# Half of an output projection's columns for one head group as seven block products, placed singly between plain pieces

## The chip, the cores and the metric

One core of one Trainium2 chip runs one transformer layer in fp32. The metric is the device time of one execution in microseconds. Three timed executions of the kernel before took 1103.21, 1103.28 and 1104.04 us; the median is 1103.28 us.

## The reference

Two groups of eight heads (width 128 each) feed one output projection, whose 2048 rows are the 1024 features of the forgetting heads (FoX) and the 1024 of the stick-breaking heads. The projection adds onto the residual stream, and a gated feed-forward network (FFN) with a short convolution follows.

```python
h = rms_norm(x, attn_norm)
p = h @ w_in                                   # q, k, v and forget gates of group A; q, k, v of group B
out_a = forgetting_attention(qa, ka, va, c)    # softmax with cumulative log-forget bias, causal
out_b = stick_breaking_attention(qb, kb, vb)
merged = concat(rms_norm(out_a, out_norm_fox), rms_norm(out_b, out_norm_sb))
x = x + merged @ w_out                         # 256 tokens, 2048 -> 2048
x = x + conv_ffn(rms_norm(x, ffn_norm))        # up 2048 -> 2 * 5632, causal conv of width 3, SiLU gate, down
```

## The kernel before, in words

**Products.** There are 256 tokens (two tiles of 128). Every fp32 weight block of 128 x 2048 elements per piece (four row blocks of 128, 512 columns) is loaded raw (`w_raw`, three buffers), rounded to a high part by ScalarE (`w_hi`, L207) and its remainder taken by VectorE (`w_lo`, L208), two buffers each in this stage. The left side (`oT`, `hT`) is held in two such parts too, and a product is the sum of high x high, low x high and high x low. `in_three` (L221) issues these matmuls, L229 in the profile: the ones with `w_hi` first, then those with `w_lo`. A plain piece of the output projection has 16 and then 8 matmuls of 128 x 512, over both token tiles.

**Output projection.** The loop at L781 goes over the two head groups, and in each over four column groups of 512. `token_major` makes one column group in two pieces of four heads each, into one accumulator `acc` (PSUM pool `psa`). Then two VectorE instructions (L803, one for each token tile) scale the accumulator by the token's RMS factor `rg` and add it onto the residual `x`. After each piece `step()` advances up to two waiting generators: the last stick-breaking heads are still running while the forgetting group's columns are projected, and `next_rows` transposes finished residual columns for the FFN (`ps_x`, L138).

**A head's rows on the engines.** A head's weights are transposed on TensorE (`ps_p`, L607) into a bank of the PSUM pool `pss` (tag "s", two banks, which the heads' scores `ps_s` and `ps_z` share). ScalarE copies them out in two instructions (L610, L611), and VectorE takes the low part from the same bank (L612, `w<-ps_p`). One step later TensorE multiplies by the values (`ps_o`, L593, L594).

**Block products elsewhere.** The down projection of the FFN already works in seven products for a 2 x 2 block of (token tiles, column groups) and two row halves: `down_in_seven`, with `bank_a`, `bank_b` and `bank_c` as one-bank accumulators, a summed weight `w_sum` (L1005), and weights that a GpSimd transfer adds onto others in place (L975, `accum_op`). Each of its products has 12 matmuls of 128 x 512.

**What sets the order.** TensorE runs in the order written. In the attention stage, VectorE, ScalarE and the queues are ordered by a scheduler; weight loads and splits get a priority of 200 (`AHEAD`) instructions. Each engine then runs its own instructions strictly in that order.

Of the kernel before, what the change touches and what calls it, by code (L numbers as in the profile page):

```python
# [2 lines left out]

# [11 lines left out]
P = 128  # L15
D = 2048
S = 256
# [28 lines left out]
def hybrid_layer(  # L46
# [31 lines left out]
    def f32(t):  # L78
        return t.bitcast(F32)
# [48 lines left out]
        nc.tensor.transpose(pp[:, :n], rows, ident[:n, :n])  # L128
        dve.tensor_copy(dst, pp[:, :n])

    hT = big.tile([P, KT, 2, S], F32R, name="hT")

    def transposed_split(k, g, n=2):

        ps = psb.tile([P, 2, S], F32, name="ps_x", tag="t")
        for j in range(n):
            for t in range(NT):
                nc.tensor.transpose(  # L138
                    ps[:, j, t * P : (t + 1) * P], xt[t][:, (k + j) * P : (k + j + 1) * P], ident
                )  # L140
        for j in range(n):
            i = k + j
            act.activation(hT[:, i, 0, :], ps[:, j, :], AF.Identity, scale=g[:, i : i + 1])
        for j in range(n):
            i = k + j
            dve.scalar_tensor_tensor(
                hT[:, i, 1, :], ps[:, j, :], g[:, i : i + 1], f32(hT[:, i, 0, :]),
                op0=ALU.mult, op1=ALU.subtract,
            )

# [46 lines left out]
    def load(src):  # L197
# [2 lines left out]
        nc.sync.dma_start(raw[:, : a * b].rearrange("p (a b) -> p a b", a=a), src)  # L200
        return raw

    def split(raw, a, b):
# [3 lines left out]
        act.copy(hi[:, :n], raw[:, :n])  # L207
        dve.tensor_tensor(lo[:, :n], raw[:, :n], f32(hi[:, :n]), op=ALU.subtract)  # L208
# [9 lines left out]
    def rows_of(w, k0, n, c0, cols):  # L218
        return w[k0 * P : (k0 + n) * P, c0 : c0 + cols].rearrange("(k p) c -> p k c", p=P)
# [14 lines left out]
    def of_half(h, part, t):  # L234
        return h[:, part, t * P : (t + 1) * P]

    def token_major(lhs, w, k0, nk, c0, cols):

        acc = psa.tile([P, NT, 512], F32, name="acc", tag="acc")
        for k in range(0, nk, 4):  # L240
            parts = weights(rows_of(w, k0 + k, 4, c0, cols), 4, cols)
            in_three(
                [acc[:, t, :cols] for t in range(NT)], parts, 4,
                lambda i, part, t: of_half(lhs(k + i), part, t), k == 0, k + 4 == nk,
            )
            step()
        return acc

    def from_features(acc, parts, kh, n=8, low_first=False):

        hi, lo = parts

        def high(k, i, j):
            nc.tensor.matmul(  # L254
                acc[:, j, :], hi[:, i, j * P : (j + 1) * P],
                hT[:, k].rearrange("p a b -> p (a b)"), start=k == 0, stop=low_first and k == KT - 1,
            )

        def low(k, i, j):
            nc.tensor.matmul(  # L260
                acc[:, j, S:], lo[:, i, j * P : (j + 1) * P], hT[:, k, 0, :],
                start=False, stop=not low_first and k == KT - 1,
            )
# [23 lines left out]
    with ExitStack() as actx:  # L287
# [7 lines left out]
        late = actx.enter_context(tc.tile_pool(name="late", bufs=1))  # L295

        def project(c0, cols):
            return token_major(lambda k: hT[:, k], wi, 0, KT, c0, cols)

        def scaled(dst, ps, t):  # L300
            act.activation(dst, ps, AF.Identity, scale=rstd1[:, t : t + 1])
# [35 lines left out]

        oT = [late.tile([P, 2, S], F32R, name=f"oT{h}") for h in range(NH)]  # L340
        vA_low = late.tile([P, WF], F32R, name="vA_low", tag="two_heads")
        done = []
        ssq = [late.tile([P, S], F32, name=f"ssq{i}") for i in range(2)]

        def attended(po, h, g, group):

            if len(done) == NH:

                two = late.tile([P, 2, 2, S], F32R, name="oT89", tag="two_heads")
                oT.extend([two[:, 0], two[:, 1]])  # L350
                oT.extend(late.tile([P, 2, S], F32R, name=f"oT{i}") for i in range(NH + 2, 2 * NH - 4))
                oT.extend(hT[:, KT - 4 + i] for i in range(4))
            done.append(group * NH + h)
            assert done[-1] == len(done) - 1
            o = oT[group * NH + h]
            act.activation(o[:, 0, :], po, AF.Identity, scale=g[:, h : h + 1])
            dve.scalar_tensor_tensor(
                o[:, 1, :], po, g[:, h : h + 1], f32(o[:, 0, :]), op0=ALU.mult, op1=ALU.subtract
            )
            if h == 0:  # L360
                act.activation(ssq[group], po, AF.Square)
            else:
                sq = tmp.tile([P, S], F32, name="osq", tag="t1", bufs=3)
                act.activation(sq, po, AF.Square)
                dve.tensor_tensor(ssq[group], ssq[group], sq, op=ALU.add)
# [19 lines left out]
        def opening():  # L385
# [37 lines left out]
            def multiply(c, i, n, high):  # L423
                hi, lo = (p[:, i : i + n] for p in parts[c])
                order = [(j, l, hi) for j in range(n) for l in range(2)] if high else [(j, 0, lo) for j in range(n)]
                for m, (j, l, r) in enumerate(order):
                    for t in range(NT):
                        nc.tensor.matmul(  # L428
                            acc[:, t, :], of_half(hT[:, 2 * c + i + j], l, t), r[:, j, :],
                            start=high and c == i == m == 0, stop=not high and c == 7 and m == n - 1,  # L430
                        )

# [93 lines left out]
        step()  # L526


        vA = (at.tile([P, WF], F32R, name="vA"), vA_low, at.tile([P, WF], F32, name="vA_t1"))

        def values(dst, acc):
            hi, lo, rest = dst
# [189 lines left out]
        def sb_head(h, qT, kT, v):  # L722
# [31 lines left out]
                yield  # L754
            attended(weighted(v, slice((h % 4) * HD, (h % 4 + 1) * HD), (w, w1)), h, g_sb, 1)

        for half in range(2):
            qT = sb_queries(half)
            kT = sb_keys(half)
# [14 lines left out]
        ss2 = const.tile([P, NT, 4], F32, name="ss2")  # L774

        def next_rows(c):
            for k in range(4 * c, 4 * c + 4, 2):
                transposed_split(k, g_ffn)
            yield

        for group in range(2):  # L781
            rg = const.tile([P, NT], F32, name=f"rg{group}")
            if group == 1:
                finish()
            for c in range(4):
                acc = token_major(lambda k: oT[group * NH + k], wo, group * NH, NH, 512 * c, 512)
                if group == c == 0:
                    assert scored[: NH + 4] == list(range(NH + 4))
                    x2 = big.tile([P, NT, D], F32, name="x2", tag="x2")
                    xt[:] = [x2[:, t, :] for t in range(NT)]  # L790
                    for t in range(NT):
                        nc.gpsimd.dma_start(xt[t], xf[t * P : (t + 1) * P, :])
                if c == 0:
                    pg = psb.tile([P, NT], F32, name="pg", tag="t")
# [5 lines left out]
                    rsqrt(rg, pg, 1.0 / WF, NT)  # L800
                for t in range(NT):
                    xs = xt[t][:, c * 512 : (c + 1) * 512]
                    dve.scalar_tensor_tensor(  # L803
                        xs, acc[:, t, :], rg[:, t : t + 1], xs, op0=ALU.mult, op1=ALU.add
                    )
# [369 lines left out]
```

## Time and profile before

| | |
|---|---|
| median of three | 1103.28 us |
| the profiled execution | 1103.81 us, of which the span from the first to the last instruction is 1102.0 us |
| TensorE busy | 1096.5 us (99%) |
| VectorE busy | 877.7 us (80%) |
| ScalarE busy | 701.9 us (64%) |
| granted TensorE clock | 1.000 |
| chain that ended last | TensorE 99% |
| stretch of the output projection | about 299.9 to 394.9 us of the span |

A profile row of a timeline reads: start, length, engine, line, operation, output <- input, shape, count, and in brackets how long the engine was idle before it and what ended that. The length of a row of several matmuls runs to the modelled end of the last, so the pitch from one matmul to the next is read from starts.

### The profile page before, as it was taken

To read this page: it belongs to the slowest core of one execution; us is meant where nothing else is said; L and a number is where in the kernel's file an instruction comes from. 1 tells how busy PE (TensorE), PEld (TensorE's weight loads), DVE (VectorE), ACT (ScalarE), POOL (GpSimd) and SP (SyncE) were. 2 spreads that over 40 slices of the span, in tenths; PEclk is the share of its full clock that TensorE was granted. 3 is DMA by queue.
4 is the path that set the end of the run, shared out by engine and by line. 5 is a ranking of instruction groups with operands and counts; after the bars stand their busy time and mean duration, and the time that the engine had idled before them with its cause. 6 is when DMAs were issued, how large, how long until landed. Compare 5 with 4: busy or idle time off the path is not lost.

```text
span 1102.0 us, 14826 instructions
## 1 busy us (share of the span) xinstructions
PE 1096.5 (99%) x5868; PEld 951.2 (86%) x5868; DVE 877.7 (80%) x941; ACT 701.9 (64%) x879; POOL 44.4 (4%) x46
## 2 busy tenths in 40 slices
PE   9999999999999999999999999999999999999998
PEld 7998888888888888888888888888888888888887
DVE  5655777975775677689889988889798889889896
ACT  6544556664653566677767776767676777677753
POOL 0000000000000000000000010100000010100010
PEclk9999999999999999999999999999999999999999
DMA  8776654576545396558989597986979689997985
GB/s 288 171 244 230 188 156 153 153 231 197 184 161 186 112 317 196 181 191 209 288 223 312 191 234 264 261 269 177 315 209 303 217 218 282 241 266 198 322 208 177
DMA packets 179407, 245.89 MB, mean 223 GB/s; under 512 B 4432, under 2 KB 119018, under 8 KB 179082
## 3 DMA queue, kind: packets, MB, share of 16 engines
q1 hardware_dynamic: 162458, 209.67, 58.6%
q0 software_dynamic: 16560, 34.75, 16.8%
q8 instruction: 46, 0.75, 0.3%
q10 hardware_dynamic: 320, 0.53, 0.1%
q14 instruction: 23, 0.19, 0.0%
HBM read 242.82 MB, written 2.11 MB: 222 GB/s over the span
## 4 chain that ended last, share of the span: by engine, by line
PE 99%; DMA 0%; DVE 0%; SPq 0%; issue 0%
PE pu L254 34%; PE acc L229 22%; PE pu L260 18%; PE bank_a L229 10%; PE bank_b L229 5%; PE bank_c L229 2%; PE acc L428 2%; PE acc L1053 1%; PE ps_x L138 1%; PE ps_o L593 1%; PE bank_a L1053 1%; PE ps_p L607 0%; DMA w_raw<-in_w_in_dram 0%; PE ps_o L594 0%; PE ps_h L307 0%; PE ps_s L522 0%
## 5 line engine op out<-in xcount | busy, mean ns | idle before, releaser
L208 DVE TENSOR_TENSOR w_lo<-w_raw,w_hi 128x2048 fp32r<-128x2048 f32 (+1 forms) x196 | 439.6, 2246 | 129.5 <-ACT w_hi L207 128.6
L207 ACT CAST w_hi<-w_raw 128x2048 fp32r<-128x2048 f32 (+1 forms) x196 | 367.3, 1877 | 235.9 <-PE acc L229 66.6
L254 PE MATMUL pu<-hT,w_hi 128*128 128x512 f32 x1664 | 394.0, 390 | 0.0
L254 PEld LDWEIGHTS pu<-hT,w_hi 128*128 128x128 f32 x1664 | 310.3, 188 | 63.2
L260 PEld LDWEIGHTS pu<-hT,w_lo 128*128 128x128 f32 x1664 | 211.9, 191 | 7.0
L260 PE MATMUL pu<-hT,w_lo 128*128 128x256 f32 x1664 | 215.1, 283 | 0.0
L229 PE MATMUL acc<-w_hi,hT 128*128 128x512 f32 (+1 forms) x576 | 124.5, 368 | 0.0
L229 PEld LDWEIGHTS acc<-w_hi,hT 128*128 128x128 f32 x576 | 101.5, 188 | 14.3
L207 ACT CAST w_hi<-w_sum 128x2048 fp32r<-128x2048 f32 x30 | 57.3, 1909 | 44.2 <-PE pu L254 36.6
L208 DVE TENSOR_TENSOR w_lo<-w_sum,w_hi 128x2048 fp32r<-128x2048 f32 x30 | 68.7, 2290 | 20.8 <-ACT w_hi L207 20.7
L870 ACT ACTIVATE tap<-up,ccol 128x256 f32<-128x256 f32 x176 | 74.6, 495 | 0.0
L229 PE MATMUL acc<-w_lo,hT 128*128 128x512 f32 (+1 forms) x288 | 64.6, 366 | 0.0
L229 PEld LDWEIGHTS acc<-w_lo,hT 128*128 128x128 f32 x288 | 51.6, 188 | 7.5
L975 POOL DMA_DIRECT2D w_sum<-in_w_down_dram x20 | 25.7, 1284 | 797.7 <-DVE w_lo L208 786.1
L229 PE MATMUL acc<-w_hi,oT 128*128 128x512 f32 x192 | 46.0, 392 | 0.0
L229 PEld LDWEIGHTS acc<-w_hi,oT 128*128 128x128 f32 x192 | 35.7, 188 | 7.3
L229 PE MATMUL bank_a<-w_hi,g 128*128 128x512 f32 x160 | 40.0, 392 | 0.0
L229 PE MATMUL bank_b<-w_hi,s 128*128 128x512 f32 x160 | 40.0, 392 | 0.0
L229 PE MATMUL bank_a<-w_hi,s 128*128 128x512 f32 x160 | 40.0, 392 | 0.0
L229 PEld LDWEIGHTS bank_b<-w_hi,s 128*128 128x128 f32 x160 | 28.9, 189 | 5.2
L229 PEld LDWEIGHTS bank_a<-w_hi,g 128*128 128x128 f32 x160 | 28.8, 189 | 5.3
L229 PEld LDWEIGHTS bank_a<-w_hi,s 128*128 128x128 f32 x160 | 28.9, 189 | 5.2
(211 smaller groups left out, 1068.7 us busy)
## 6 DMA issues: line engine op xcount, KB each, us to landing
w_raw<-in_w_up_dram SPq DMA_DIRECT2D x88, 1024.0 KB, 7.5
w_raw<-in_w_down_dram SPq DMA_DIRECT2D x44, 1024.0 KB, 6.4
w_raw<-in_w_in_dram SPq DMA_DIRECT2D x36, 1024.0 KB, 5.4
w_sum<-in_w_down_dram POOLq DMA_DIRECT2D x20, 1024.0 KB, 9.9
w_raw<-in_w_out_dram SPq DMA_DIRECT2D x16, 1024.0 KB, 5.1
w_raw<-in_w_down_dram POOLq DMA_DIRECT2D x10, 1024.0 KB, 14.9
w_raw<-in_w_in_dram SPq DMA_DIRECT2D x12, 688.0 KB, 4.2
w_raw<-in_w_in_dram SPq DMA_DIRECT2D x6, 512.0 KB, 6.8
```

The source lines that it names most:

```text
L138: nc.tensor.transpose(ps[:, j, t * P : (t + 1) * P], xt[t][:, (k + j) * P : (k + j + 1) * P], ident)
L207: act.copy(hi[:, :n], raw[:, :n])
L208: dve.tensor_tensor(lo[:, :n], raw[:, :n], f32(hi[:, :n]), op=ALU.subtract)
L229: nc.tensor.matmul(o, lhs(i, l, t), r[:, i, :], start=starts and j == 0, stop=stops and j == 3 * n - 1, skip_group_check=more,)
L254: nc.tensor.matmul(acc[:, j, :], hi[:, i, j * P : (j + 1) * P], hT[:, k].rearrange("p a b -> p (a b)"), start=k == 0, stop=low_first and k ...
L260: nc.tensor.matmul(acc[:, j, S:], lo[:, i, j * P : (j + 1) * P], hT[:, k, 0, :], start=False, stop=not low_first and k == KT - 1,)
L428: nc.tensor.matmul(acc[:, t, :], of_half(hT[:, 2 * c + i + j], l, t), r[:, j, :], start=high and c == i == m == 0, stop=not high and c == ...
L593: nc.tensor.matmul(po, v[j][:, hs], wp[:, k], start=i == 0, stop=False)
L870: act.activation(taps[w][:, j, :], u[:, j, w : w + S], AF.Copy, scale=ccol[:, w, f : f + 1])
L975: nc.gpsimd.dma_start(mem[into][:, : nk * 512].rearrange("p (a b) -> p a b", a=nk), src, accum_op=ALU.add)
L1053: nc.tensor.matmul(o, of_half(g, l, t), r[:, i, c0 : c0 + cols], start=kh == 0 and j == 0, stop=kh == n - 1 and j == 11,)
```

## The change

For the forgetting heads, the column groups 2 and 3 (columns 1024 to 2047) are no longer made by `token_major` in four plain pieces (96 matmuls of 128 x 512). They become a 2 x 2 block (token tiles by column groups, with two halves of four heads inside) made by `in_seven`, in seven products of 12 matmuls (84). The plain pieces that are left are the forgetting heads' columns 0 and 1 and all of the stick-breaking heads' columns, and `token_major` takes one product out of the generator `seven` behind each of its pieces. The first two calls only pass (the first issues two loads), so the seven products stand behind the third to the ninth plain piece.

Seven products need sums on both sides. `block_sums` makes sums of the heads' outputs on VectorE (six instructions, in the stretch of the second half's keys), and `block_parts` splits them into high and low (two ScalarE, two VectorE instructions). On the weight side, one VectorE addition makes `w_sum` from w11 and w12, and three GpSimd transfers add w22, w22 and w21 in place. Two weight tiles are loaded into freed memory (`w_sum` where the values of the forgetting heads were, `x12` in a quarter of `hT`, which is now four tiles). Each product is accumulated in one bank of `pss`, the pool with tag "s" that the heads' `ps_z` and `ps_p` use. `in_turn` keeps the weight splits in the order of the program, and `in_order` pins the sums. Behind column group 1 of the second head group, two `next_rows` run in a chain in place of one each behind groups 0 and 1.

```diff
+    def residual(t, c, ps, factor):
+        xs = xt[t][:, c : c + 512]
+        dve.scalar_tensor_tensor(xs, ps, factor[:, t : t + 1], xs, op0=ALU.mult, op1=ALU.add)
+    def in_seven(c0, plus_rg, minus_rg):
+        w11, w12, w21, w22 = (rows_of(wo, 4 * h, 4, c0 + 512 * i, 512) for h in range(2) for i in range(2))
...
+        def product(bank, lhs, parts, to, factor=plus_rg):
+            new = bank not in banks
+            if new:
+                banks[bank] = pss.tile([P, 512], F32, name=bank, tag="s")
+            in_three([banks[bank]], parts, 4, lhs, new, True, more=not new)
+            residual(to[0], c0 + 512 * to[1], banks[bank], factor)
...
+        with tc.high_priority(offset=AHEAD):
+            for into, src in ((w, w11), (x12, w12)):
+                nc.sync.dma_start(into.rearrange("p (a b) -> p a b", a=4), src)
+        yield
+        yield
+        with tc.high_priority(offset=AHEAD):
+            parts = split(w, 4, 512)
+        in_order(dve.tensor_tensor(w, w, x12, op=ALU.add))
+        product("bank_a", of_heads(0, 0), parts, (0, 0))
+        yield
+        block_parts()
+        product("bank_c", of_heads(1, 0), weights(w21, 4, 512), (0, 0))
+        yield
+        with tc.high_priority(offset=AHEAD):
+            parts = split(w, 4, 512)
+        plus(w, w22)
+        plus(x12, w22)
+        product("bank_b", of_sums(0, 1), parts, (1, 1))
+        yield
+        product("bank_b", of_sums(1, 0), weights(w22, 4, 512), (0, 1))
+        yield
+        with tc.high_priority(offset=AHEAD):
+            parts = split(w, 4, 512)
+        plus(w, w21)
+        product("bank_a", of_sums(1, 1), parts, (0, 1), minus_rg)
+        yield
+        with tc.high_priority(offset=AHEAD):
+            parts = split(x12, 4, 512)
+        product("bank_a", of_sums(0, 0), parts, (1, 1), minus_rg)
+        yield
+        with tc.high_priority(offset=AHEAD):
+            parts = split(w, 4, 512)
+        product("bank_a", of_heads(1, 1), parts, (1, 0))
...
-            for c in range(4):
-                acc = token_major(lambda k: oT[group * NH + k], wo, group * NH, NH, 512 * c, 512)
+            for c in range(4 if group else 2):
+                acc = token_major(
+                    lambda k: oT[group * NH + k], wo, group * NH, NH, 512 * c, 512,
+                    seven,
+                )
...
-                    waiting.append(next_rows(c))
+                    if c == 1:
+                        waiting.append(chain(next_rows(0), next_rows(1)))
+                    elif c > 1:
+                        waiting.append(next_rows(c))
```

Two places show what this does to the engines' orders.

**TensorE where the first of the seven is put.** Before, behind the first piece of the forgetting heads' column group 1, two heads' weights are transposed (`ps_p`, three matmuls a head) and the next plain piece follows:

```order
L229 MATMUL acc_2963<-w_lo_2967,oT2_100 128x512 x2
L229 MATMUL acc_2963<-w_lo_2967,oT3_101 128x512 x2
L607 MATMUL ps_p_2994<-cs_70,e_2886 128x128 x3
L607 MATMUL ps_p_3003<-cs_70,e_2903 128x128 x3
L229 MATMUL acc_2963<-w_hi_3014,oT4_102 128x512 x4
L229 MATMUL acc_2963<-w_hi_3014,oT5_103 128x512 x4
```

Now the first product stands there, in `bank_a`:

```order
L245 MATMUL acc_2973<-w_hi_2976,oT_fox_101 128x512 x16
L245 MATMUL acc_2973<-w_lo_2977,oT_fox_101 128x512 x8
L626 MATMUL ps_p_3004<-cs_70,e_2891 128x128 x3
L626 MATMUL ps_p_3013<-cs_70,e_2908 128x128 x3
L245 MATMUL bank_a_3027<-w_hi_3022,oT_fox_101 128x512 x8
L245 MATMUL bank_a_3027<-w_lo_3023,oT_fox_101 128x512 x4
L245 MATMUL acc_2973<-w_hi_3043,oT_fox_101 128x512 x16
```

The plain piece moved behind it. `ps_p_3004` and `ps_p_3013` hold the two banks of the pool, and `bank_a` is the third tile asked of it: its first matmul waits for VectorE, for the instruction that reads `ps_p_3004` last (`w<-ps_p`).

**VectorE at the same place.** Before (`rs_a` and `rs_u` are small steps of the RMS factor `rg`, `e` the heads' weights before transposition):

```order
L748 TENSOR_TENSOR e<-e,masks 128x2x128 x2
L111 TENSOR_SCALAR rs_a<-pg 128x2
L208 TENSOR_TENSOR w_lo<-w_raw,w_hi 128x2048
L114 TENSOR_TENSOR rs_u<-rs_a,rs_y 128x2
L612 TENSOR_TENSOR w<-ps_p,w 128x256
L115 TENSOR_TENSOR rs_u<-rs_u,rs_y 128x2
```

Now:

```order
L767 TENSOR_TENSOR e<-e,masks 128x2x128 x2
L112 TENSOR_SCALAR rs_a<-pg 128x2
L868 TENSOR_TENSOR w_sum<-w_sum,x_2921 128x2048
L221 TENSOR_TENSOR w_lo<-w_raw,w_hi 128x2048
L115 TENSOR_TENSOR rs_u<-rs_a,rs_y 128x2
L631 TENSOR_TENSOR w<-ps_p,w 128x256
L116 TENSOR_TENSOR rs_u<-rs_u,rs_y 128x2
```

The addition for `w_sum` came in ahead of the split. The reading of `ps_p` keeps its place behind the split of a later piece's weights.

**VectorE in the second half's keys.** Before (`ssq` sums squares of the heads' outputs, `t` is the projected pair of heads):

```order
L685 TENSOR_TENSOR q_parts<-t_2470,q_parts 128x256
L208 TENSOR_TENSOR w_lo<-w_raw,w_hi 128x2048
L365 TENSOR_TENSOR ssq_108<-ssq_108,osq 128x256 x2
L284 TENSOR_TENSOR t_2554<-pu,t_2554 128x512
L678 SCALAR_TENSOR_TENSOR t_2554<-t_2554,R_1503 128x512
L208 TENSOR_TENSOR w_lo<-w_raw,w_hi 128x2048
```

Now:

```order
L704 TENSOR_TENSOR q_parts<-t_2465,q_parts 128x256
L784 TENSOR_TENSOR oT_blocks_2472<-oT_fox 128x1024
L221 TENSOR_TENSOR w_lo<-w_raw,w_hi 128x2048
L383 TENSOR_TENSOR ssq_104<-ssq_104,osq 128x256
L784 TENSOR_TENSOR oT_blocks_2474<-oT_fox 128x1024
L383 TENSOR_TENSOR ssq_104<-ssq_104,osq 128x256
L788 TENSOR_TENSOR oT_blocks_2472<-oT_blocks_2472 128x4x128
L789 TENSOR_TENSOR oT_blocks_2472<-oT_blocks_2472,oT_blocks_2474 128x4x128
L790 SCALAR_TENSOR_TENSOR oT_blocks_2474<-oT_blocks_2472,oT_blocks_2474 128x4x128
L301 TENSOR_TENSOR t_2557<-pu,t_2557 128x512
L791 TENSOR_TENSOR oT_blocks_2474<-oT_blocks_2474 128x4x128
L697 SCALAR_TENSOR_TENSOR t_2557<-t_2557,R_1498 128x512
```

The six sums of `block_sums` came in around the split and the steps of the next pair of keys.

More of the change, by code (lines that the diff above doesn't have):

```diff
@@ L2 @@
 from contextlib import ExitStack, nullcontext
+from itertools import chain
 import concourse.bass as bass
@@ L129, in columns, with new_tokens @@
         dve.tensor_copy(dst, pp[:, :n])
-    hT = big.tile([P, KT, 2, S], F32R, name="hT")
+    hT = [None] * KT
+    def new_tokens(g):
+        t = big.tile([P, 4, 2, S], F32R, name=f"hT{g}", tag=f"hT{g}")
+        hT[4 * g : 4 * g + 4] = [t[:, i] for i in range(4)]
+    for g in range(4):
+        new_tokens(g)
     def transposed_split(k, g, n=2):
@@ L206, in split @@
         n = a * b
-        act.copy(hi[:, :n], raw[:, :n])
-        dve.tensor_tensor(lo[:, :n], raw[:, :n], f32(hi[:, :n]), op=ALU.subtract)
+        with ExitStack() as turn:
+            for ins in in_turn:
+                turn.enter_context(tc.issue_after(ins.ins))
+            last = [act.copy(hi[:, :n], raw[:, :n])]
+            last.append(dve.tensor_tensor(lo[:, :n], raw[:, :n], f32(hi[:, :n]), op=ALU.subtract))
+        last_split[:] = last
+        if in_turn:
+            in_turn[:] = last
         return (
@@ L246, in token_major @@
             step()
+            next(behind, None)
         return acc
@@ L255, in high @@
                 acc[:, j, :], hi[:, i, j * P : (j + 1) * P],
[L256 removed]
+                hT[k].rearrange("p a b -> p (a b)"), start=k == 0, stop=low_first and k == KT - 1,
             )
@@ L336, in fox_rows @@
             yield
-        oT = [late.tile([P, 2, S], F32R, name=f"oT{h}") for h in range(NH)]
-        vA_low = late.tile([P, WF], F32R, name="vA_low", tag="two_heads")
+        oT_fox = late.tile([P, NH, 2, S], F32R, name="oT_fox")
+        oT = [oT_fox[:, h] for h in range(NH)]
+        vA_rest = late.tile([P, WF], F32, name="vA_rest", tag="two_heads")
         done = []
@@ L351, in attended @@
                 oT.extend(late.tile([P, 2, S], F32R, name=f"oT{i}") for i in range(NH + 2, 2 * NH - 4))
-                oT.extend(hT[:, KT - 4 + i] for i in range(4))
+                oT.extend(hT[KT - 4 + i] for i in range(4))
             done.append(group * NH + h)
@@ L755, in sb_head, with block_sums, block_parts @@
             attended(weighted(v, slice((h % 4) * HD, (h % 4 + 1) * HD), (w, w1)), h, g_sb, 1)
+        in_order = tc.keep_in_program_order
+        blocks, sums = [], []
+        def block_sums():
+            for h, tag in enumerate(("minus_c1", "blocks")):
+                blocks.append(at.tile([P, 4, S], F32, name=f"oT_blocks{h}", tag=tag))
+                some = slice(4 * h, 4 * h + 4)
+                in_order(dve.tensor_tensor(
+                    blocks[h], f32(oT_fox[:, some, 0, :]), f32(oT_fox[:, some, 1, :]), op=ALU.add
+                ))
+            a11, a21, a12, a22 = (blocks[h][:, :, t * P : (t + 1) * P] for h in range(2) for t in range(2))
+            in_order(dve.tensor_tensor(a11, a11, a21, op=ALU.subtract))
+            in_order(dve.tensor_tensor(a21, a21, a22, op=ALU.subtract))
+            in_order(dve.scalar_tensor_tensor(a22, a11, -1.0, a22, op0=ALU.mult, op1=ALU.subtract))
+            in_order(dve.tensor_tensor(a12, a12, a22, op=ALU.add))
+        def block_parts():
+            sums.extend(big.tile([P, NH, S], F32R, name="oT_sums", tag=f"hT{g}") for g in (1, 2))
+            places = [[t[:, 4 * h : 4 * h + 4] for t in sums] for h in range(2)]
+            for (hi, _), block in zip(places, blocks):
+                in_order(act.copy(hi, block))
+            for (hi, lo), block in zip(places, blocks):
+                in_order(dve.tensor_tensor(lo, block, f32(hi), op=ALU.subtract))
         for half in range(2):
             qT = sb_queries(half)
+            if half:
+                block_sums()
             kT = sb_keys(half)
@@ L779, in next_rows, with of_heads, of_sums, plus @@
             yield
-        for group in range(2):
-            rg = const.tile([P, NT], F32, name=f"rg{group}")
+        def residual(t, c, ps, factor):
[3 more added lines that the diff above has]
+            w11, w12, w21, w22 = (rows_of(wo, 4 * h, 4, c0 + 512 * i, 512) for h in range(2) for i in range(2))
+            banks = {}
+            def of_heads(h, t):
+                return lambda i, part, _: of_half(oT[4 * h + i], part, t)
+            def of_sums(h, t):
+                return lambda i, part, _: sums[part][:, 4 * h + i, t * P : (t + 1) * P]
+            def plus(into, src):
+                with tc.high_priority(offset=AHEAD):
+                    nc.gpsimd.dma_start(
+                        into.rearrange("p (a b) -> p a b", a=4), src, accum_op=ALU.add
+                    )
[5 more added lines that the diff above has]
+                residual(to[0], c0 + 512 * to[1], banks[bank], factor)
+            w, x12 = (
+                pool.tile([P, 2048], F32, name=name, tag=tag)
+                for pool, name, tag in ((at, "w_sum", "vA"), (big, "x12", "hT0"))
+            )
+            with tc.high_priority(offset=AHEAD):
[28 more added lines that the diff above has]
+            yield
+            with tc.high_priority(offset=AHEAD):
+                parts = split(w, 4, 512)
+            product("bank_a", of_heads(1, 1), parts, (1, 0))
@@ L783, in hybrid_layer @@
+        rgs = [const.tile([P, NT], F32, name=f"rg{group}") for group in range(2)]
+        minus_rg = const.tile([P, NT], F32, name="minus_rg")
+        seven = in_seven(1024, rgs[0], minus_rg)
+        in_turn.extend(last_split)
+        for group, rg in enumerate(rgs):
             if group == 1:
                 finish()
-            for c in range(4):
-                acc = token_major(lambda k: oT[group * NH + k], wo, group * NH, NH, 512 * c, 512)
+            for c in range(4 if group else 2):
+                acc = token_major(
+                    lambda k: oT[group * NH + k], wo, group * NH, NH, 512 * c, 512,
+                    seven,
+                )
```

26 lines of the change are left out of this document (15 added, 11 removed).

## The prediction

> **What bounds the kernel now.** I read the page first: busy times and the chain that ended last.
>
> ```profile
> span 1102.0 us, 14826 instructions
> PE 1096.5 (99%) x5868; PEld 951.2 (86%) x5868; DVE 877.7 (80%) x941; ACT 701.9 (64%) x879; POOL 44.4 (4%) x46
> PE 99%; DMA 0%; DVE 0%; SPq 0%; issue 0%
> ```
>
> TensorE is the bound from end to end. So a matmul taken away is worth its pitch, and any wait that TensorE gets is paid in full, since nothing later has slack to give it back. Next, whom TensorE waits for, in the whole span (columns: in total, times, longest):
>
> ```profile
> PE idle L381 <- DVE zeros L371: 1.1, 1, 1.1
> PE acc L428 <- DVE w_hi L409: 1.1, 1, 1.1
> PE ps_x L138 <- DMA x<-in_x_dram: 0.2, 1, 0.2
> ```
>
> All three lie in the first 7 us. In the output projection TensorE never waits; the change has to keep that. Then the room on the helpers there, from windows (PE, PEld, DVE, ACT, POOL busy, clock, DMA share, GB/s):
>
> ```profile
> 290.00:320.00 30.00, 30.00 (x152) 25.35 (x151) 20.12 (x25) 17.69 (x28) 0.00 (x0) 1.00 0.48 157
> 320.00:350.00 30.00, 30.00 (x139) 24.98 (x138) 19.50 (x23) 11.98 (x13) 0.00 (x0) 1.00 0.60 194
> 350.00:380.00 30.00, 30.00 (x144) 25.05 (x143) 18.95 (x22) 15.44 (x23) 0.00 (x0) 1.00 0.44 141
> ```
>
> VectorE has about 31 us free of 90, ScalarE 45. Room in sum is there; what decides is who stands behind whom.
>
> **The change part by part.** *Matmuls taken away.* Pitches come from the chain in order of time (start, length, what):
>
> ```profile
> 326.53 32.67 PE acc L229 x144
> 527.17 2.75 PE bank_a L229 x12
> ```
>
> A plain matmul takes 32.67 / 144 = 0.227 us, the 96 that go are 21.8 us. A block product of 12 matmuls takes 2.75 us in the FFN, seven are 19.25 us. The gain is 21.8 - 19.25 = 2.5 us (2.7 if the new ones run at the plain pitch).
>
> *Work added to the helpers.* From the page and the tile `w_sum`:
>
> ```profile
> L207 ACT CAST w_hi<-w_sum 128x2048 fp32r<-128x2048 f32 x30 | 57.3, 1909 | 44.2 <-PE pu L254 36.6
> L208 DVE TENSOR_TENSOR w_lo<-w_sum,w_hi 128x2048 fp32r<-128x2048 f32 x30 | 68.7, 2290 | 20.8 <-ACT w_hi L207 20.7
> L1005 DVE TENSOR_TENSOR w_sum<-w_raw x10: 2283/2284/2292, 493.5 to 1049.8; 128x2048 f32<-128x2048 f32 x10
> ```
>
> Seven splits in place of four: ScalarE 3 x 1.91 = 5.7 us, VectorE 3 x 2.29 = 6.9 us, and one weight sum of 2.28 us. In the new rhythm a plain piece (24 x 0.227 = 5.44 us) and a product (2.75 us) make 8.19 us, against two splits: 3.82 us on ScalarE, 4.58 us on VectorE. With two buffers, the high part of the next plain piece can begin when the 16 high matmuls of this one are through (3.63 us) and ends near 3.7 + 1.9 = 5.6 us, 2.6 us before it is needed; its low part begins at 5.5 us, ends at 7.8 us and is needed at 8.19 + 3.63 us. So the steady rhythm costs TensorE nothing: splits are hidden by the matmuls of the piece and product before.
>
> *The first product, bank_a.* Here the order makes a wait. This is the place in the trace of before, TensorE, then ScalarE, then VectorE:
>
> ```profile
> 319.06 0.82 PE L607 MATMUL ps_p<-cs,e 128*128 128x128 f32 x6
> 319.63 3.91 PE L229 MATMUL acc<-w_hi,oT 128*128 128x512 f32 x16
> ...
> 317.85 1.89 ACT L207 CAST w_hi<-w_raw 128x2048 fp32r<-128x2048 f32 x1
> ...
> 317.55 0.15 DVE L111 TENSOR_SCALAR rs_a<-pg 128x2 f32<-128x2 f32 x1
> 319.77 2.29 DVE L208 TENSOR_TENSOR w_lo<-w_raw,w_hi 128x2048 fp32r<-128x2048 f32 x1 [2.07 <-ACT w_hi L207]
> 321.98 0.15 DVE L114 TENSOR_TENSOR rs_u<-rs_a,rs_y 128x2 f32<-128x2 f32 x1
> 322.05 0.42 DVE L612 TENSOR_TENSOR w<-ps_p,w 128x256 fp32r<-128x256 f32 x1
> ```
>
> Up to here the two programs run alike (the same pieces of 24, the same heads). TensorE is through with `ps_p` at 319.63, and before it went on into `acc`, another pool. Now `bank_a` wants the bank of the first `ps_p`, which VectorE reads last in `w<-ps_p`. That read already ended as late as 322.47, because the split of a later piece stands ahead of it; nobody cared. Now the weight sum comes in at 317.62, fills the idle 2.07 us and ends its turn at 317.62 + 2.21 = 319.83 (2.21 us is the pitch from 319.77 to 321.98); the split starts 0.06 us later than before, `w<-ps_p` ends at 322.53, and TensorE starts about 322.6. It stands idle for 322.6 - 319.63 = 3.0 us. Lower bound: 322.47 - 319.63 = 2.8 us, if the sum cost nothing at all; upper: 3.5 us, if another half microsecond of small steps goes ahead of it. I take 3.0. Queued behind the waiting `bank_a` on TensorE is everything else, so it is paid in full. The other six products ask for a bank whose last readers (`x` additions, or a `ps_p` two pieces back) are long done.
>
> What such a gap does to the clock: the longest gap in the trace is 1.1 us (the waits above), and the granted clock is 1.00 in every window quoted. [...] A 3.0 us gap is not shown in this trace, so I keep it as a rival.
>
> *Sums of the heads' outputs.* `block_parts` stands ahead of the third product. Between the first two products lie a plain piece and two heads' `ps_o`, which take 1.1 us:
>
> ```profile
> 325.20 0.41 PE L593 MATMUL ps_o<-w,vB 128*128 128x256 f32 x2
> ...
> 326.29 3.91 PE L229 MATMUL acc<-w_hi,oT 128*128 128x512 f32 x16
> ```
>
> So the second product runs from 322.6 + 2.75 + 5.44 + 1.1 = 331.9, and the third from 331.9 + 2.75 + 5.44 = 340.1 us. Its cast of `w_sum` waits for the second's high matmuls (331.9 + 8 x 0.229 = 333.7, begun near 333.9), its `w_lo` ends near 338.1, two `ssq` (0.95 us, row at 262.03 below) and the first low part of the sums (1.2 us, below) end near 340.2 us. TensorE needs that for its second matmul, at 340.3. I take 0, with 0.3 us as the upper end. `block_sums` stands here:
>
> ```profile
> 258.47 0.41 DVE L685 TENSOR_TENSOR q_parts<-t,q_parts 128x256 fp32r<-128x256 f32 x1
> 259.82 2.29 DVE L208 TENSOR_TENSOR w_lo<-w_raw,w_hi 128x2048 fp32r<-128x2048 f32 x1 [0.94 <-ACT w_hi L207]
> 262.03 0.95 DVE L365 TENSOR_TENSOR ssq<-ssq,osq 128x256 f32<-128x256 f32 x2
> 265.99 0.69 DVE L284 TENSOR_TENSOR t<-pu,t 128x512 f32<-128x512 f32 x1 [3.01 <-ACT t L283]
> 266.72 0.69 DVE L678 SCALAR_TENSOR_TENSOR t<-t,R 128x512 f32<-128x512 f32 x1
> 267.80 2.29 DVE L208 TENSOR_TENSOR w_lo<-w_raw,w_hi 128x2048 fp32r<-128x2048 f32 x1 [0.39 <-ACT w_hi L207]
> 268.75 4.00 PE L260 MATMUL pu<-hT,w_lo 128*128 128x256 f32 x32
> ```
>
> No row has 1024 elements; between 0.69 us (512) and 2.29 us (2048) it is 1.2 us. Two of those and four of 0.69 are 5.2 us, against idle of 0.94 + 3.01 + 0.39 = 4.3 us and some overlap: the `w_lo` of 267.80 moves to about 268.1 and ends at 270.4. TensorE needs it for the second half of the 32 low matmuls, at 268.75 + 16 x 0.12 = 270.67. Cover of 0.3 us is left; without it the cost is the shortfall, some tenths. I take 0, upper end 0.3 us.
>
> *Transfers.* Three in-place additions on GpSimd are new, none in the way of another there (its next work is in the FFN). Their kind, from the tiles `w_sum` and `w_raw`:
>
> ```profile
> DMA to landing us min/median/max: 8.5/9.9/14.1
> DMA to landing us min/median/max: 4.1/6.5/18.4
> ```
>
> The sum for the fifth product is issued when the third's low part is made, about 2 us ahead of its matmuls, and is due one cast (1.9 us) ahead of the fifth: two periods, 16.7 us. For the seventh it is 17.5 us. Both hold 9.9 and 14.1. The first load of `w_sum` on SP waits for the last use of the values, and behind it is a weight load that was issued here:
>
> ```profile
> 208.55 0.49 PE L593 MATMUL ps_o<-pT,vA 128*128 128x256 f32 x2
> ...
> 210.75 0.37 SPq L200 DMA_DIRECT2D w_raw<-in_w_in_dram  x1
> ```
>
> The values are free at 209.0, so the load behind is not held up. Cost 0.
>
> *Sum.* -2.5 + 3.0 + 0 + 0 = +0.5 us. The profiled execution took 1103.81 us (span 1102.0, 1.8 us around it), 0.53 us above the median, and would come to 1104.3; on the median of 1103.28 that is 1103.8 us. A difference of 0.2%, 2.2 us, is about what a measurement of this kernel can tell from no change.
>
> **The rivals.** *The gain stays whole.* The wait at `bank_a` would have to be under half a microsecond: VectorE would have to read `ps_p` before it starts the split. Against it are the fixed order and the end at 322.47 even before; for it, only that the sum of helper work is small. 1103.3 - 2.5 = 1100.8 us, chance 0.13.
>
> *The clock falls in the gap (slower).* Place: behind the 3.0 us at `bank_a`. It decides from the gap length at which the clock is taken back; the trace clears 1.1 us only. Nearest rows: nothing (as after 1.1 us), up to half pitch through the product behind the gap, 12 x 0.229 = 2.7 us more. 1103.8 + 2.7 = 1106.5 us, chance 0.11. [...]
>
> *A sum of weights lands late (slower).* Place: the cast for the fifth or seventh product, from a landing above 16.7 us. The slowest of `w_raw` took 18.4, which would cost 1.7 + 0.9 = 2.6 us: 1106.4 us. The DMA share there is 0.44 to 0.60, so that is unlikely: 0.08.
>
> **How the numbers follow.** The forecast has 0.68, with a range of its own of 1102.9 (gain 2.7, gap 2.8, less what a run scatters) to 1105.0 (gap 3.5, 0.3 and 0.3 for the sums). Faster by over 0.2% is the first rival, 0.13; slower the other two, 0.19; the rest, 0.68, is within 0.2%. The range from 1100.6 to 1105.6 takes in the forecast and the first rival, and of the slower ones only the mild form.
>
> **What would show it.**
>
> ```profile
> 394.87 1.98 PE L254 MATMUL pu<-hT,w_hi 128*128 128x512 f32 x8
> ```
>
> Right: TensorE has one wait of about 3 us, at the first matmul of `bank_a` on VectorE's `w<-ps_p`, near 319.6 us; everything after it stands within 1 us of before, with the FFN's first matmul 0.5 us later than in this row, near 395.4; seven products at 2.7 to 2.8 us. Wrong: no such wait, or other waits above 0.5 us, named at `oT_sums`, at a cast of `w_sum`, or at 270 us. Longer matmuls or a granted clock under 1.00 right after the gap would be the second rival.

## The result, and the profile after

The changed kernel took 1105.12 us (median of 21 executions, 1103.90 to 1107.09), the kernel before 1103.53 us (21 executions beside it, 1103.06 to 1104.65): a ratio of 1.0015, 95% interval 1.0009 to 1.0022. That is slower by 1.6 us, and in the median less than the 0.2% that I had set as the bound of no change (the interval's upper end, 0.22%, is just past it). The forecast was 1103.8 us.

The median hides two kinds of executions. Each lists the mean granted clock of its core (the share of its full clock that TensorE was given; 1.000 is all of it). In 6 of 21 it is 1.000, and these took 1103.90 to 1104.78 us (median 1104.1). In 15 it is 0.998 or 0.997, and these took 1105.04 to 1107.09 us (median 1105.5). The profiled execution is of the first kind (1103.9 us, clock 1.000), so what it shows is the forecast's own case. Its page:

```profile
span 1102.1 us, 14836 instructions
PE 1095.1 (99%) x5856; PEld 949.7 (86%) x5856; DVE 895.4 (81%) x957; ACT 709.4 (64%) x884; POOL 47.9 (4%) x49
```

Twelve matmuls fewer (7 x 12 in place of 96), TensorE busy for 1.4 us less, and the span is the same. Whom TensorE waits for (in total, times, longest):

```profile
PE idle L399 <- DVE zeros L389: 1.1, 1, 1.1
PE bank_a L245 <- DVE w L631: 2.7, 1, 2.7
```

The first is the wait at the start that the kernel before has too. The second is new. The place, TensorE first, then VectorE:

```profile
318.65 0.82 PE L626 MATMUL ps_p<-cs,e 128*128 128x128 f32 x6
322.15 2.11 PE L245 MATMUL bank_a<-w_hi,oT_fox 128*128 128x512 f32 x8 [2.68 <-DVE w L631]
...
317.21 2.28 DVE L868 TENSOR_TENSOR w_sum<-w_sum,x 128x2048 f32<-128x2048 f32 x1
319.41 2.28 DVE L221 TENSOR_TENSOR w_lo<-w_raw,w_hi 128x2048 fp32r<-128x2048 f32 x1
321.68 0.42 DVE L631 TENSOR_TENSOR w<-ps_p,w 128x256 fp32r<-128x256 f32 x1
```

`bank_a` starts as soon as VectorE has read the first `ps_p`, and that stands behind the split, as forecast. The two other places that I had marked, the sums of the heads' outputs (VectorE makes `oT_sums`, TensorE uses it) and `block_sums`:

```profile
338.71 2.36 DVE L799 TENSOR_TENSOR oT_sums<-oT_blocks,oT_sums 128x1024 fp32r<-128x1024 f32 x2
339.83 2.03 PE L245 MATMUL bank_b<-w_hi,oT_sums 128*128 128x512 f32 x8
...
267.39 2.29 DVE L221 TENSOR_TENSOR w_lo<-w_raw,w_hi 128x2048 fp32r<-128x2048 f32 x1
268.34 4.00 PE L277 MATMUL pu<-hT,w_lo 128*128 128x256 f32 x32
```

Neither row of TensorE has a wait. To measure the stage alone, I take the time from the heads' `ps_p` near 246 us, ahead of the change's new work on TensorE, VectorE and ScalarE, to the FFN's first matmul; what an execution gains or loses ahead of it (0.4 us between these two) then drops out. Before (its second row is in the prediction, at 394.87) and after:

```profile
246.38 1.01 PE L607 MATMUL ps_p<-cs,e 128*128 128x128 f32 x6
```

```profile
245.99 1.00 PE L626 MATMUL ps_p<-cs,e 128*128 128x128 f32 x6
394.77 1.98 PE L271 MATMUL pu<-hT,w_hi 128*128 128x512 f32 x8
```

Before it took 394.87 - 246.38 = 148.49 us, after 394.77 - 245.99 = 148.78 us: +0.3 us where the clock holds. The median of the whole executions at 1.000 is 0.6 us above the kernel before (1104.1 - 1103.5); the other 0.3 us is not in this stage of the profiled executions, and where it comes from stays open.

### The profile page after: what moved, and what is told of

It reads as the page before. It is cut to its first block, busy times and chain, and to the rows that moved or that the text cites. A ratio compares the mean times of both kernels' runs of the same rounds, so it can differ in the third digit from the quotient of the medians.

```text
span 1102.1 us, 14836 instructions
## 1 busy us (share of the span) xinstructions
PE 1095.1 (99%) x5856; PEld 949.7 (86%) x5856; DVE 895.4 (81%) x957; ACT 709.4 (64%) x884; POOL 47.9 (4%) x49
## 3 DMA queue, kind: packets, MB, share of 16 engines
HBM read 245.97 MB, written 2.11 MB: 225 GB/s over the span
## 4 chain that ended last, share of the span: by engine, by line
PE 99%; DVE 0%; issue 0%
PE pu L271 34%; PE acc L245 20%; PE pu L277 18%; PE bank_a L245 11%; PE bank_b L245 5%; PE bank_c L245 3%; PE acc L446 2%; PE acc L1177 1%; PE ps_x L146 1%; PE ps_o L612 1%; PE bank_a L1177 1%; PE ps_p L626 0%; PE idle L399 0%; PE ps_o L613 0%; PE ps_h L324 0%; PE ps_s L540 0%
## 5 line engine op out<-in xcount | busy, mean ns | idle before, releaser
L221 DVE TENSOR_TENSOR w_lo<-w_raw,w_hi 128x2048 fp32r<-128x2048 f32 (+1 forms) x194 | 435.1, 2246 | 120.8 <-ACT w_hi L220 120.0
L220 ACT CAST w_hi<-w_raw 128x2048 fp32r<-128x2048 f32 (+1 forms) x194 | 363.6, 1877 | 224.1 <-PE acc L245 61.7
L220 ACT CAST w_hi<-w_sum 128x2048 fp32r<-128x2048 f32 x34 | 64.9, 1909 | 48.7 <-PE pu L271 36.5
L221 DVE TENSOR_TENSOR w_lo<-w_sum,w_hi 128x2048 fp32r<-128x2048 f32 x34 | 77.8, 2290 | 22.0 <-ACT w_hi L220 22.0
L999 DVE TENSOR_TENSOR val<-val,tap 128x512 f32<-128x512 f32 x44 | 30.3, 689 | 2.7 <-DVE val L999 0.5
L999 DVE TENSOR_TENSOR gate<-gate,tap 128x512 f32<-128x512 f32 x44 | 30.3, 689 | 2.5 <-ACT tap L994 0.2
```

The source lines that it names most:

```text
L220: last = [act.copy(hi[:, :n], raw[:, :n])]
L221: last.append(dve.tensor_tensor(lo[:, :n], raw[:, :n], f32(hi[:, :n]), op=ALU.subtract))
L999: dve.tensor_tensor(a, a, tap, op=ALU.add)
```

## The experiments

My theory: the wait for the bank eats the gain, and TensorE's idleness in it lets the clock fall in most executions (15 of 21). The rivals: the clock falls, or time is lost, for another reason (the single products, the transfers).

**TensorE kept busy in the wait.** Ahead of the first product, into a free bank:

```
+            filler = psb.tile([P, S], F32, name="filler", tag="t")
+            for _ in range(22):
+                nc.tensor.matmul(filler, zeros[:, :P], zeros, start=True, stop=True)
             product("bank_a", of_heads(0, 0), parts, (0, 0))
```

> The changed kernel, with 22 matmuls of zeros (256 columns, bf16, about 0.11 us each: some 2.5 us) on TensorE between the last `ps_p` and the first matmul of `bank_a`, into a free bank; the wait for the bank stays, but TensorE is not idle in it. Theory (the wait of 2.7 us eats the gain, and the idle gap lets the clock fall in most executions): the granted clock is 1.000 in all executions, about 1104.1 us, as the undisturbed executions of the changed kernel (1103.9 to 1104.8). Rival (the clock falls for another reason: the single products, or the added transfers): 0.998 in most executions and about 1105.1 us, as before this edit. If zeros don't count as work: the same as the rival.

Measured: 1103.45 us (1103.35 to 1103.92), clock 1.000 in 11 of 11; ratio to before 1.0000 (0.9992 to 1.0009). From its timeline:

```profile
245.74 1.00 PE L626 MATMUL ps_p<-cs,e 128*128 128x128 f32 x6
...
319.06 2.57 PE L871 MATMUL filler<-zeros 128*128 128x256 bf16 x22
321.90 2.14 PE L245 MATMUL bank_a<-w_hi,oT_fox 128*128 128x512 f32 x8 [0.28 <-DVE w L631]
...
394.54 1.98 PE L271 MATMUL pu<-hT,w_hi 128*128 128x512 f32 x8
```

Counted from the `ps_p` near 246 us, the product starts no earlier: 321.90 - 245.74 = 76.16 us, and 322.15 - 245.99 = 76.16 us without the zeros. The clock's loss is gone. So it was the idleness, not the products and not the transfers, which are all still there. The median is 0.65 us below the 1104.1 us expected. The stage takes 394.54 - 245.74 = 148.80 us, as without the zeros (148.78), so that difference, too, lies outside the stage and stays open.

**Shorter gaps.** The same with 12 and with 6 of these matmuls.

> As the kernel with 22 matmuls of zeros, with 12: TensorE's idle gap is about 1.3 us in place of 2.7, the wait's end stays where it was. Theory, where the point of decision lies over 1.3 us: clock 1.000 in all executions, 1104.1 us; where it lies lower, or where idle time adds up in any amount, the clock falls in some or most, 1105 us. Rival (another reason than the gap): 0.998 in most, 1105.1 us.

> As the kernel with 22 matmuls of zeros, with 6: an idle gap of about 2.0 us, between 1.3 (clock kept in 11 of 11) and 2.7 (lost in 15 of 21). Theory with a sharp point of decision: lost in all or in none. [...] Time 1103.8 us where kept, 1.0 to 1.7 us more where lost.

Measured: with 12, 1103.79 us, clock 1.000 in 10 of 11 and 0.999 in one, which was no slower (1103.70 us; some executions of the kernel before show 0.999 too); ratio 1.0001 (0.9993 to 1.0010). With 6, 1104.95 us, ratio 1.0010 (1.0001 to 1.0019), and two kinds again: 5 of 11 at 1.000 with 1103.56 to 1103.86 us, 6 of 11 at 0.998 with 1104.95 to 1105.39 us. The gap with 12, and then with 6, whose profiled execution lost the clock:

```profile
322.41 1.89 PE L245 MATMUL bank_a<-w_hi,oT_fox 128*128 128x512 f32 x7 [1.37 <-DVE w L631]
```

```profile
321.81 3.68 PE L245 MATMUL bank_a<-w_hi,oT_fox 128*128 128x512 f32 x8 [2.03 <-DVE w L631]
325.31 1.10 PE L245 MATMUL bank_a<-w_lo,oT_fox 128*128 128x512 f32 x4
```

The gap of 1.4 us cost the clock in 0 of 11 executions, that of 2.0 us in 6 of 11: with the same program it goes either way from execution to execution. These few counts alone don't show that 6 of 11 is a smaller share than the 15 of 21 at 2.7 us. Eight matmuls almost wholly at half clock took 3.68 us in place of 2.11.

**A longer gap.** One VectorE operation more ahead of the sum of weights:

```
+            in_order(dve.tensor_tensor(x12[:, :1024], x12[:, :1024], x12[:, :1024], op=ALU.max))
             in_order(dve.tensor_tensor(w, w, x12, op=ALU.add))
```

> The changed kernel with one VectorE operation more (1024 elements, 1.22 us, a maximum of x12 with itself, which changes nothing) ahead of the sum of weights: the wait at `bank_a` grows from 2.7 to about 3.9 us. Theory (the gap decides on the clock): the clock falls in all executions, 0.998 or lower, and the profile shows a granted clock below 1.00 behind the gap; 1105.3 + 1.2 = 1106.5 us, with few or none at 1105.3 (1104.1 + 1.2). Rival (the clock has nothing to do with the gap): the same share of executions at 1.000 as without the edit (6 of 21), 1105.1 + 1.2 = 1106.3 us, a third of them at 1105.3.

Measured: 1107.09 us (1106.28 to 1107.58), clock 0.998 or 0.997 in 6 of 6; ratio 1.0033 (1.0020 to 1.0045). The theory's number is missed by 0.6 us: the three executions at 0.998 took 1106.28 to 1106.69 us, the three at 0.997 1107.50 to 1107.58 us. The wait in its timeline, and windows of 1 us behind it (the granted clock is the third column from the right):

```profile
323.52 3.33 PE L245 MATMUL bank_a<-w_hi,oT_fox 128*128 128x512 f32 x8 [3.94 <-DVE w L631]
```

```profile
323.00:324.00 1.00, 0.48 (x2) 0.44 (x3) 0.96 (x7) 0.00 (x0) 0.00 (x0) 1.00 0.55 61
324.00:325.00 1.00, 1.00 (x5) 0.77 (x4) 0.97 (x4) 0.00 (x0) 0.00 (x0) 0.53 0.94 156
325.00:326.00 1.00, 1.00 (x4) 0.81 (x3) 0.65 (x1) 0.00 (x0) 0.00 (x0) 0.50 1.14 209
326.00:327.00 1.00, 1.00 (x3) 0.80 (x3) 0.00 (x0) 0.11 (x1) 0.00 (x0) 0.50 1.12 211
327.00:328.00 1.00, 1.00 (x5) 0.73 (x4) 0.00 (x0) 1.00 (x1) 0.00 (x0) 0.76 1.09 256
328.00:329.00 1.00, 1.00 (x6) 0.82 (x5) 0.83 (x2) 0.79 (x1) 0.00 (x0) 1.00 1.06 252
```

TensorE is at work again from 323.52, yet the clock falls only at 324.06 (0.53 = 0.06 + 0.94 / 2) and comes back at 327.48, with 0.50 in the windows between: 3.42 us at half clock, 1.71 us lost. Here the clock was lost every time. By itself, 6 of 6 would not rule out the rival's share (15 in 21 each would give that 13 times in 100); the kernels with shorter gaps, where the share goes to nothing (0 of 11 at 1.4 us), do.

**The wait without the change.** The kernel before, with one matmul of zeros that asks for the same bank:

```
             w, w1 = transposed_weights(e, "w")
+            if h == 7:
+                hold = pss.tile([P, S], F32, name="hold", tag="s")
+                nc.tensor.matmul(hold, zeros[:, :P], zeros, start=True, stop=True)
```

> The kernel before, with one matmul of zeros into a bank of the same pool right behind the last `ps_p`: the wait for the bank without products, weight sums or new transfers. VectorE's `w<-ps_p` ended 2.8 us after TensorE was through with `ps_p` there too. Theory (the bank's wait does not need the new weight sum, and the gap brings the clock down): a wait of 2.8 us, 1103.5 + 2.8 = 1106.3 us where the clock holds, 1.0 to 1.7 us more in most executions. Rival 1 (the weight sum on VectorE makes the wait): much less than 2.8 us. Rival 2 (the clock falls for the products' sake): 2.8 us, but clock 1.000 in all executions.

Measured: 1107.51 us (1106.38 to 1108.21), ratio 1.0036 (1.0024 to 1.0049); 2 of 5 executions at 1.000 with 1106.38 and 1106.55 us, 3 of 5 at 0.998 with 1107.51 to 1108.21 us. Its timeline:

```profile
318.51 0.81 PE L607 MATMUL ps_p<-cs,e 128*128 128x128 f32 x6
321.96 0.27 PE L754 MATMUL hold<-zeros 128*128 128x256 bf16 x1 [2.64 <-DVE w L612]
321.99 5.51 PE L229 MATMUL acc<-w_hi,oT 128*128 128x512 f32 x16
```

The same wait (2.64 us) and the same two kinds, with no product, no sum of weights and no new transfer. So the added sum (L868) does not make the wait: it fills a hole, and the split behind it was late already.

**The first product one place later.** Behind the fourth plain piece, where the two `ps_p` have long been read:

```
             yield
             yield
+            yield
             with tc.high_priority(offset=AHEAD):
                 parts = split(w, 4, 512)
...
             product("bank_a", of_heads(0, 0), parts, (0, 0))
-            yield
             block_parts()
```

> The changed kernel with its first product one place later: behind the fourth plain piece, together with the second product, where the two `ps_p` have long been read; all other products where they were. Theory (the bank's wait is all that eats the gain): no wait at `bank_a`, clock 1.000 in all executions, the products' 2.5 us show: 1101.0 us (1100.5 to 1101.6), faster than both kernels. Rival 1 (the loss is not the bank's, or comes back at another place): 1103.5 to 1105 us. Rival 2 (the clock falls for the products' sake): 0.998 in most executions, 1102.1 us.

Measured: 1106.03 us (1104.08 to 1107.10), ratio 1.0021 (1.0012 to 1.0030), clock under 1.000 in 10 of 11. My theory's number was missed by 5 us; rival 1's sort of thing happened, with a fall of the clock on top of it. Its new wait, in total and on TensorE, and VectorE at the place:

```profile
PE bank_b L245 <- DVE x L831: 3.4, 1, 3.4
...
340.67 3.61 PE L245 MATMUL bank_b<-w_hi,oT_sums 128*128 128x512 f32 x8 [3.37 <-DVE x L831]
```

```profile
333.90 2.29 DVE L221 TENSOR_TENSOR w_lo<-w_sum,w_hi 128x2048 fp32r<-128x2048 f32 x1
336.10 0.42 DVE L383 TENSOR_TENSOR ssq<-ssq,osq 128x256 f32<-128x256 f32 x1
336.44 1.22 DVE L799 TENSOR_TENSOR oT_sums<-oT_blocks,oT_sums 128x1024 fp32r<-128x1024 f32 x1
337.57 2.29 DVE L221 TENSOR_TENSOR w_lo<-w_raw,w_hi 128x2048 fp32r<-128x2048 f32 x1
339.78 0.75 DVE L831 SCALAR_TENSOR_TENSOR x<-bank_c,rg,x 128x512 f32<-128x512 f32 x1
```

The wait at `bank_a` is gone, and the same wait has come up at `bank_b`, which takes over the bank of `bank_c`: its reader now stands behind the splits. My expectation had looked at one bank only.

**The same, with that reader ahead of the splits.** On top of the edit before:

```
-                residual(to[0], c0 + 512 * to[1], banks[bank], factor)
+                with tc.high_priority(offset=2 * AHEAD) if bank == "bank_c" else nullcontext():
+                    residual(to[0], c0 + 512 * to[1], banks[bank], factor)
```

> As the kernel with the first product one place later, and the addition of the second product to `x` (`x<-bank_c`) put ahead of the splits on VectorE; in the run without that, it stood behind three splits and the third product waited 3.4 us for it. Theory (the waits for banks are all that eats the gain, and gaps over some 2 us bring the clock down): no wait of TensorE in the output projection, clock 1.000 in all executions, 1103.5 - 2.5 = 1101.0 us (1100.5 to 1101.6). Rival (the products cost something that is not a wait: clock, transfers, weight loads): 1102 us or more without a wait in the trace.

Measured: 1100.83 us (1100.41 to 1101.09), ratio 0.9976 (0.9968 to 0.9985), clock 1.000 in 10 of 11 and 0.999 in the fastest. It is faster than both kernels, by 2.5 us than the one before. The start's 1.1 us is TensorE's only wait, and the stage:

```profile
245.85 1.01 PE L626 MATMUL ps_p<-cs,e 128*128 128x128 f32 x6
391.71 1.98 PE L271 MATMUL pu<-hT,w_hi 128*128 128x512 f32 x8
```

145.86 us against 148.49 before: the gain of the seven products by itself is 2.63 us. The one execution of the version before this that kept its clock took 1104.08 us, 3.25 us more than this median, which is about its wait of 3.4 us.

**The bank freed by ScalarE.** The changed order, with one step changed for the last two heads (`copy` is their `e`, else nothing):

```
-        def transposed_weights(e, name):
+        def transposed_weights(e, name, copy=None):
...
             pt0 = pt[:, 0:2, :].rearrange("p a b -> p (a b)")
+            if copy is not None:
+                act.copy(copy, pt)
+                pt, pt0 = copy, copy[:, 0:2, :].rearrange("p a b -> p (a b)")
             act.copy(w[:, 0], pt0)
...
-            w, w1 = transposed_weights(e, "w")
+            w, w1 = transposed_weights(e, "w", e if h >= 6 else None)
```

> The changed kernel, in its own order; for the last two heads ScalarE copies `ps_p` whole to SBUF first, and the other steps (ScalarE's and VectorE's `w<-ps_p`) read that copy. So the bank is free when ScalarE is done (a first copy of 384 elements, about 0.45 us from 319.3), and no longer waits for VectorE's split. Theory (VectorE's late read of the bank is the cause): the wait at `bank_a` falls from 2.7 to about 0.6 us, clock 1.000 in all executions, 1104.1 - 2.1 = 1102.0 us; between both kernels' forecast of the whole gain (1101.0) and before. Rival (the wait is set by something else, such as the weights of the first product): 2.7 us remain, 1104 to 1105 us.

Measured: 1101.40 us (1101.13 to 1102.30), ratio 0.9984 (0.9975 to 0.9993), clock 1.000 in 10 of 11 and 0.999 in one; 0.6 us below the theory's number. ScalarE's copies, and TensorE:

```profile
319.57 0.84 ACT L630 COPY e<-ps_p 128x384 f32<-128x384 f32 x2
```

```profile
320.09 2.12 PE L245 MATMUL bank_a<-w_hi,oT_fox 128*128 128x512 f32 x8 [0.38 <-ACT e L630]
```

With all else in place (the order, the sum of weights, the transfers), the late read of the bank is what decides whether the gain shows.

## Why the prediction was right, and where it was not

*The gain.* Forecast 2.5 us, or 2.7 at the plain pitch; the stage without waits gives 2.63 us. In the changed kernel the seven products took 2.72 to 2.87 us each, from the first matmul of one to the matmul that follows it, against the forecast 2.7 to 2.8.

*The wait.* Forecast 3.0 us (2.8 to 3.5), at the first matmul of `bank_a`, on `w<-ps_p`. Its row gives 2.68 us, counted from the modelled end of the last `ps_p` matmul. The forecast counted from the time at which the next matmul starts where nothing holds it, 0.57 us behind the first `ps_p` matmul in the kernel before (319.63 - 319.06). Counted that way it is 322.15 - (318.65 + 0.57) = 2.93 us, and by stages, against the version without the wait, it is 0.29 + 2.63 = 2.92 us: the forecast was 0.1 us off. The forecast of +0.5 us for the sum stands against +0.3 us. The cause was put right in both halves: the split delays the read, and the added sum of weights costs next to nothing.

*The terms at nothing.* No wait at `oT_sums`, none at 268 us, none at a cast of `w_sum`. The covers held.

*The clock.* This is the step that failed. I gave the fall of the clock 0.11 and priced it at up to 2.7 us, the whole product at half pitch. It happened in 15 of 21 executions, and the median lies in it: 1105.12 us instead of the 1104.1 of the executions without it. The price was twice too high (1105.5 - 1104.1 = 1.4 us between the two medians; 1.7 us where the half-clock stretch lies wholly in work), the chance far too low. That the whole product behind the gap runs at half pitch was an assumption of mine: no run shows its 2.7 us, and none stands behind the mild form of this rival in the range either. What the profiled executions show in its place is half clock for 3.42 us, which cost 1.71 us with the longer gap. What misled me was to think of one gap length from which the clock is lost, and to hold it for likely above 3.0 us. No run shows such a length: the clock was lost in 0 of 11 executions at a gap of 1.4 us, in 6 of 11 at 2.0 us and in 15 of 21 at the 2.7 us of this kernel.

*The whole.* The difference stayed within 0.2%, and the time within the range from 1100.6 to 1105.6 us, but of the 1.6 us only the smaller part is the forecast's sum: +0.3 us by the stage, +0.6 us by the medians at 1.000. The larger part, 1.0 us in the median, belongs to a rival. The forecast's own range ended at 1105.0 us, just below the median of 1105.12 us. That the time stayed in the wider range is in part luck: two errors met, the chance of the rival too low and its price too high, and at that price (1106.5 us) the median would have lain outside. The first rival (the gain whole) needed VectorE to read `ps_p` ahead of the split. The kernel in which ScalarE frees the bank shows that the late read was indeed what stood against it; a VectorE that reads first was not run for this bank. The third rival (a late transfer) did not happen: TensorE has no such wait. Of its price of 2.6 us, 0.9 us had no row behind it, and no run here gives one.

## What to carry to other kernels

Before a matmul is put at a new place, look up who last reads the bank that it takes over, and what stands ahead of that reader on its engine; a bank can be held by a step that nobody waited for until then (here `w<-ps_p`, a wait of 2.7 us). Moving the matmul may just move the wait to the next bank (3.4 us at `bank_b` here): check each bank that changes hands, and free it with the engine that has room. On a kernel bound by TensorE, price an idle gap of 2 us or more with the clock's share too (here 6 of 11 executions lost the clock at 2.0 us, and one stretch at half clock cost 1.71 us), and look at the clock of every execution, since one profile shows only one kind.

## What the runs showed of the hardware that I had not expected

The clock's loss by the idle gap, from the waits and the clocks above (for the changed kernel 2.68 us, one place later 3.37, the longer gap 3.94; the gaps in one execution of each):

| Gap, us | 0.3 | 1.4 | 2.0 | 2.6 | 2.7 | 3.4 | 3.9 |
|---|---|---|---|---|---|---|---|
| Executions at 0.998 or below | 0 of 11 | 0 of 11 | 6 of 11 | 3 of 5 | 15 of 21 | 10 of 11 | 6 of 6 |

From none at 1.4 us the share grows to all at 3.9 us; at the gaps from 2.0 to 3.4 us one and the same kernel lost the clock in some executions and kept it in others. What share a gap between 1.4 and 2.0 us would have, and what decides in a single execution, no run shows.

The stretch at half clock had nearly the same length in all four profiled executions that lost the clock, with gaps from 2.0 to 3.9 us: 3.42 us with the longer gap (324.06 to 327.48, above), 3.40 to 3.42 us in the three others. The windows in which it fell and came back with 6 matmuls of zeros, then for the wait without the change, and then for the first product one place later:

```profile
321.00:322.00 1.00, 0.19 (x1) 0.19 (x2) 1.00 (x5) 0.00 (x0) 0.04 (x1) 0.97 0.16 23
325.00:326.00 1.00, 1.00 (x5) 0.80 (x4) 0.00 (x0) 0.47 (x1) 0.00 (x0) 0.83 1.10 252
```

```profile
323.00:324.00 1.00, 1.00 (x5) 0.77 (x4) 1.00 (x2) 0.00 (x0) 0.00 (x0) 0.66 0.62 233
326.00:327.00 1.00, 1.00 (x4) 0.77 (x4) 0.00 (x0) 0.00 (x0) 0.00 (x0) 0.63 0.00 0
```

```profile
340.00:341.00 1.00, 0.33 (x1) 0.36 (x2) 1.00 (x2) 0.00 (x0) 0.00 (x0) 0.91 1.11 205
344.00:345.00 1.00, 1.00 (x5) 0.78 (x4) 0.00 (x0) 0.68 (x1) 0.00 (x0) 0.88 1.04 348
```

(Read with a clock of 1.00 or 0.50 and nothing between, as the windows on either side show it, 0.97 puts the fall at 321.94 and 0.83 the return at 325.34. The others fell at 323.32 and 340.82 and came back at 326.74 and 344.24, each 3.42 us later.) In all four the clock fell only when TensorE was at work again: 0.13 us after the start of the matmul that had waited (321.81) with 6 matmuls of zeros, 1.36 us (321.96) for the wait without the change, 0.15 us (340.67) one place later and 0.54 us (323.52) with the longer gap. The two executions of the changed kernel at 0.997 took 1.6 and 1.8 us more than the median of those at 0.998 (1105.29 us), those with the longer gap about 1 us more. An estimate from the 1.71 us above: one such loss is 0.0016 of the whole and shows as 0.998, two are 0.0031 and show as 0.997, so a second stretch at half clock would fit. None of these executions was profiled, so it stays open.
